# Four weight sums of a seven-product pair on VectorE, and a planner rule for the port that it shares with GpSimd

## The chip, the core and the metric

The kernel runs on one core of a Trainium2 chip. The metric is the device time of one execution in microseconds; for each kernel the median of the runs is given. Besides these there is one profiled execution, whose trace has the start and length of every instruction. Five engines work side by side, each through its own queue in order: TensorE (PE; its weight loads are listed apart as PEld), VectorE (DVE), ScalarE (ACT), GpSimd (POOL) and SyncE (SP), which here issues the DMA transfers.

## The reference

Two layers of an encoder on x (1, 512, 1024) in float32, with a memory of 256 tokens. Each layer adds three blocks to x:

```python
x += concat(neighbourhood_attention(h), gqa_attention(h)) @ w_out      # h = rms_norm(x)
x += memory_cross_attention(rms_norm(x), rms_norm(mem))                # 4 heads
x += conv_ffn(rms_norm(x))

def conv_ffn(h, w_up, conv_w, conv_b, w_down):
    u = h @ w_up                                   # (512, 2 x 2816)
    up = pad(u, one position on each side)
    u = up[:, :-2] * conv_w[0] + up[:, 1:-1] * conv_w[1] + up[:, 2:] * conv_w[2] + conv_b
    gate, val = split(u, 2)
    return (silu(gate) * val) @ w_down
```

A last RMSNorm follows. The change touches the product `h @ w_up` of the ConvFFN.

## The kernel before, in words

**Tiling.** x is kept transposed: eight tiles `xT` of 128 features by 512 positions. A float32 product is made exact enough by splitting both operands into a high part (a copy rounded to a TensorE format, on ScalarE) and a low part (operand minus high part, on VectorE or GpSimd), and issuing three matmuls: high by high, high by low, low by high. So every weight tile that a DMA brings as `raw` needs a copy and a subtraction before TensorE can use it.

**Seven products.** The hidden 2816 features make 22 blocks of 128. For each, gate and value are two products over 1024 features. Blocks 0 to 5 (`N_PLAIN = 6`) do them plainly. Blocks 6 to 21 do both at once as a two-by-two block product in Strassen's manner, with seven products of half the width instead of eight: 16 such pairs in each layer, 32 in all. `take_pair` fetches two raw weight tiles (128 x 1024 each), `combined` (L573 to L589) makes of them the seven weight operands: `11`, `12` and `22` are halves of the raw tiles, and four are sums,

```python
s1 = first[:, 4:8] + second[:, 0:4]        s3 = first[:, 0:4] + second[:, 0:4]
s2 = s3 + first[:, 4:8]                    s4 = s2 + second[:, 4:8]
```

each an add on 128 x 512 float32. All seven are then split (copy on ScalarE, subtraction on VectorE). `SUMS` (L506) names the engine of the four adds, GpSimd. `up` (L1603) issues the seven `product`s (L1589, 12 matmuls of 256 columns each) in the order 11, s1, s2, 12, s4, s3, 22; between them stand the matmuls of a block of the second FFN product, `down_grouped`, whose results are added into `xT`. `up_finish` (L1633) does convolution taps, SiLU and the product of the two sides on ScalarE and VectorE.

**Buffers.** `raw` has three slots (`N_RAW = 3`); the tiles `t` (sums among them) fourteen. A slot that comes free lets SyncE issue the next transfer.

**The order of the work.** No instruction is issued where it is written. Each call is put on a `Tape` as a `Step`, with its reads, writes, an estimated duration, and `shared`, which is true for GpSimd steps of more than 8 columns and for VectorE steps whose inputs are both in SBUF (and for some copies). `plan` lists candidate orders: it calls `run`, a list scheduler, with six settings of `PLANS` and four rounds each, replays each order six times with disturbed durations, and keeps the one with the least mean end. `play` then issues all steps in that order at one line (L405 of before, L408 of the changed kernel), so all rows of the profile have this line and are told apart by their tile names. An engine's order is thus fixed when the program is built.

In `run`, an engine's candidates are the steps whose inputs are done; each has an earliest start `t` from its data (`ready`), its engine (`free`) and free slots. Among those that could start within `patience` of the first, the one with the earliest due time is picked. When a `shared` step is picked while the other engine still has the port, it is lengthened by what is left of that, less `GRACE` (140 ns); `pool` and `vector` hold the end of the last shared step on GpSimd and VectorE.

Of the kernel before, what the change touches and what calls it, by code (L numbers as in the profile page):

```python
# [72 lines left out]
E_PE, E_ACT, E_DVE, E_POOL, E_SP = ENGINES  # L73
HANDOVER, LANDING, IN_FLIGHT, GRACE = 40.0, 1800.0, 8, 140.0
# [27 lines left out]
class Step:  # L102
# [5 lines left out]
    def __init__(self, i, engine, name, call, args, kwargs):  # L108
        self.i, self.engine, self.name, self.call = i, engine, name, (call, args, kwargs)
        self.reads, self.writes = [], []  # L110
        for n, a in [*enumerate(args), *kwargs.items()]:
            if hasattr(a, "tensor") or type(a).__name__ == "Tile":
                a = a if hasattr(a, "ap") and not callable(a.ap) else a[:]
                (self.writes if n in (0, "out", "accum_out") else self.reads).append(a)
        self.needs, self.frees, self.after, self.leads = set(), set(), set(), set()
        self.opens, self.tiles, self.moved = [], [], 0
        if name == "dma_start":
            self.busy = self.length = 450.0
            to, source = self.writes[0], self.reads[0] if self.reads else None
            runs = min(run(a) for a in (to, source) if a is not None)  # L120
            inside = source is not None and type(source.tensor).__name__ == type(to.tensor).__name__ == "Tile"
            rate = 205.0 if to.shape[0] < P or inside else 285.0 if runs < 256 else 340.0 if runs < 512 else 375.0
            self.moved = 4 / rate
            for c in to.shape:
                self.moved *= c
        elif name == "make_identity":
            self.busy = self.length = 1200.0
        else:
            self.busy, self.length = self.times()
        ends = self.reads[:: max(1, len(self.reads) - 1)] if name in TWO_INPUTS else self.reads[:1] + self.writes  # L130
        self.shared = engine == E_POOL and columns(self.writes[0]) > 8 or (
            engine == E_DVE and (name in TWO_INPUTS or name in FAST and (name == "tensor_copy" or columns(self.writes[0]) > 4))
            and all(tag_of(a.tensor) not in IN_PSUM for a in ends))
# [48 lines left out]
class Tape:  # L182
# [87 lines left out]
    def run(self, due, rank, patience, ahead, margin=0.0, aside={}, order=None, rng=None):  # L270


        steps = self.steps
        todo = [len(s.needs) + len(s.after) for s in steps]
        start, ready, free = [-1.0] * len(steps), [0.0] * len(steps), [0.0] * 5
# [14 lines left out]
        pool = vector = memory = 0.0  # L290
        flying = [0.0] * IN_FLIGHT

        def room(s):
            t = 0.0
            for x in s.opens:
                tag = self.tag[x]
                n = len(slots[tag])
                if not n or not order and x != waiting[tag][0] and (n <= aside.get(tag, n) or x not in waiting[tag][:5]):
                    return None
                t = max(t, min(slots[tag]))  # L300
            return t

        for _ in steps:
            best = None
            for e in ENGINES:
                if order or e == E_PE:
                    while head[e] < len(program[e]) and start[program[e][head[e]]] >= 0:
                        head[e] += 1
                    if head[e] == len(program[e]):
                        continue  # L310
                if order:
                    i = program[e][head[e]]
                    among = (i,) if not todo[i] else ()
                elif e == E_PE:
                    reach = rank[program[e][min(head[e] + ahead, len(program[e]) - 1)]]
                    among = [i for i in open_to[e] if rank[i] <= reach]
                else:
                    among = open_to[e]
                can = []
                for i in among:  # L320
                    t = room(steps[i]) if steps[i].opens else 0.0
                    if steps[i].moved and t is not None:
                        t = max(t, flying[-IN_FLIGHT])
                    if t is not None:
                        can.append((max(t, ready[i], free[e]), i))
                if can:
                    soon = min(can)[0] + patience[e]
                    _, t, i = min((due[i] if due and e != E_PE else rank[i], t, i) for t, i in can if t <= soon)
                    if best is None or t < best[0]:
                        best = t, i  # L330
            if best is None:
                return None
            t, i = best
            s = steps[i]
            busy = s.busy * slow[i]
            if s.shared and s.engine == E_POOL:
                busy += max(0.0, vector - t - GRACE)
                pool = t + busy
            elif s.shared:
                busy += max(0.0, pool - t - GRACE)  # L340
                vector = t + busy
            start[i], free[s.engine] = t, t + busy
            end = t + busy + s.length - s.busy + late[i]
            if s.moved:
                memory = max(memory, t + busy) + s.moved
                end = memory + LANDING + (12.0 * late[i] if rng is None else 1500.0 * rng.random())
                flying.append(end)
            taken.append(i)
            open_to[s.engine].remove(i)
            for x in s.opens:  # L350
                tag = self.tag[x]
                slots[tag].remove(min(slots[tag]))
                waiting[tag].remove(x)
            for x in s.tiles:
                left[x] -= 1
                ends[x] = max(ends.get(x, 0.0), end)
                if not left[x]:
                    slots[self.tag[x]].append(ends[x] + HANDOVER)
            for x in s.frees:
                q = steps[x]  # L360
                same = q.engine == s.engine and not s.moved
                ready[x] = max(ready[x], t if same and s.engine == E_PE else end + (30.0 if same else HANDOVER))
                todo[x] -= 1
                if not todo[x]:
                    open_to[q.engine].append(x)
            for x in s.leads:
                ready[x] = max(ready[x], t)
                todo[x] -= 1
                if not todo[x]:
                    open_to[steps[x].engine].append(x)  # L370
# [129 lines left out]
def encoder_kernel(ctx: ExitStack, tc: tile.TileContext, t: dict, out: list):  # L500
    nc = tc.nc
    tape = Tape()
    PE, ACT, DVE, POOL, SP = (
        Taped(tape, e, calls) for e, calls in zip(ENGINES, (nc.tensor, nc.scalar, nc.vector, nc.gpsimd, nc.sync)))
    late = Late(PE)
    LO_A, SUMS, LO_S = DVE, POOL, DVE  # L506
# [15 lines left out]
    def rtile(shape, dt=F32R):  # L522
        return rpool.tile([P, *shape], dt, tag="r", name=nm("r"), padded_shape=[P, *pad(shape)])
# [12 lines left out]
    def tmp(shape=(S,)):  # L536
        return tpool.tile([P, *shape], F32, tag="t", name=nm("t"))
# [13 lines left out]
    plan, raws, ready = [], [], []  # L551
# [15 lines left out]
    def operand_of(v, tile, sub):  # L567

        w = tile.rearrange("p (n k) c -> p n k c", n=2)
        ACT.copy(w[:, 0], v)  # L570
        sub.tensor_sub(w[:, 1], v, f(w[:, 0]))
        return [(w[:, 0, k], w[:, 1, k]) for k in range(4)]

    def wtile(tag):
        return wpool.tile([P, KC, P], F32R, tag=tag, name=nm(tag))

    def combined(first, second, early):

        parts = {}
        for n, v in (("11", first[:, 0:4]), ("12", second[:, 4:8]), ("22", first[:, 4:8])):  # L580
            parts[n] = operand_of(v, rtile((8, P)), LO_A)
        sums = {n: tmp((4, P)) for n in ("s3", "s1", "s2", "s4")}
        SUMS.tensor_add(sums["s1"], first[:, 4:8], second[:, 0:4])
        SUMS.tensor_add(sums["s3"], first[:, 0:4], second[:, 0:4])
        SUMS.tensor_add(sums["s2"], sums["s3"], first[:, 4:8])
        SUMS.tensor_add(sums["s4"], sums["s2"], second[:, 4:8])
        for n, tag in (("s1", "hi"), ("s2", "lo"), ("s4", "hi"), ("s3", "lo")):
            parts[n] = operand_of(sums[n], rtile((8, P)) if early else wtile(tag), LO_S)
        return parts  # L589
# [76 lines left out]
    first = nc.const_aps.tensor(0.0, (P, P), F32)  # L666
# [1299 lines left out]
```

## Time and profile before

| what | value |
|---|---|
| median of 3 runs | 1300.8 us (1300.58 to 1301.65) |
| span of the profiled execution | 1300.8 us |
| its own time | 1302.85 us |
| TensorE busy | 1290.8 us, 99% |
| VectorE busy | 1076.1 us, 83% |
| ScalarE busy | 784.4 us, 60% |
| GpSimd busy | 659.5 us, 51% |
| granted TensorE clock | 0.998 |

The span is the time between the first and the last instruction of the trace. A row of the timeline gives the start, the length in us, the engine, the line, the operation, output<-inputs by tile name, shapes, and the count of rows that were joined; in brackets the idle time of the engine just before, and what ended it. A row of a group gives total busy time, mean ns of one, idle time before, and its releaser. For the tile names: `mm`, `sc` and `tr` are PSUM banks, `r`, `hi`, `lo` and `xg` hold split operands, `t` and `s` are scratch.

### The profile page before, as it was taken

How to read it: one execution, taken by the hardware profiler on the slowest of the kernel's cores; microseconds unless marked ns; L12 is line 12 of the kernel's file. 1: busy time of each engine (PE TensorE's matmuls, PEld its weight loads, DVE VectorE, ACT ScalarE, POOL GpSimd, SP SyncE). 2: the span in 40 equal slices, each digit the busy share in tenths (PEclk: the TensorE clock that was granted, in tenths of full speed). 3: DMA queues.
4: the chain of work that ended last, by engine and by line, in shares of the span. 5: the costliest groups of instructions: out<-in, count | busy, mean ns of one | idle time of the engine just before them, and what ended most of it. 6: DMA issues, size and time to landing. Idle time of an engine off the chain costs nothing.

```text
span 1300.8 us, 20807 instructions
## 1 busy us (share of the span) xinstructions
PE 1290.8 (99%) x7557; PEld 1138.5 (88%) x7557; DVE 1076.1 (83%) x2001; ACT 784.4 (60%) x1526; POOL 659.5 (51%) x527
## 2 busy tenths in 40 slices
PE   9999999999999999999999999999999999999998
PEld 7898888888899999999888988888888999999997
DVE  7689885769999999888555897956799999997884
ACT  7776786555665555554537866865646555554552
POOL 4565857716823534433726566765365333452360
PEclk9999999999999999999999999999999999999999
DMA  8741313313224333223355322232132233323231
GB/s 286 224 141 49 105 56 98 98 35 113 81 82 123 105 113 115 66 98 123 112 162 179 115 80 82 65 99 96 49 98 81 82 115 115 128 99 98 97 99 66
DMA packets 42902, 137.48 MB, mean 106 GB/s; under 512 B 5040, under 2 KB 8496, under 8 KB 42800
## 3 DMA queue, kind: packets, MB, share of 16 engines
q1 hardware_dynamic: 42224, 135.51, 32.9%
q8 instruction: 59, 0.97, 0.3%
q10 hardware_dynamic: 576, 0.66, 0.1%
q14 instruction: 43, 0.35, 0.1%
HBM read 126.18 MB, written 2.10 MB: 99 GB/s over the span
## 4 chain that ended last, share of the span: by engine, by line
PE 91%; DVE 5%; issue 2%; POOL 2%; ACT 1%; DVEq 0%; POOLq 0%; ACTq 0%
PE mm L405 52%; PE tr L405 20%; PE sc L405 19%; DVE t L405 2%; DVE r L405 1%; POOL lo L405 1%; DVE lo L405 0%; DVE s L405 0%; POOL s L405 0%; POOL t L405 0%; ACT r L405 0%; ACT t L405 0%; DVE mm L405 0%; DVE xg L405 0%; DVE hi L405 0%
## 5 line engine op out<-in xcount | busy, mean ns | idle before, releaser
L405 POOL TENSOR_TENSOR lo<-raw,hi 128x512 fp32r<-128x512 f32 (+2 forms) x164 | 255.9, 1579 | 161.6 <-ACT hi L405 153.9
L405 PE MATMUL mm<-xg,hi 128*128 128x512 f32 (+1 forms) x930 | 289.7, 392 | 0.0
L405 POOL TENSOR_TENSOR t<-raw,raw 128x512 f32<-128x512 f32 x64 | 99.1, 1569 | 284.2 <-DMA raw<-in_w 231.1
L405 ACT CAST hi<-raw 128x512 fp32r<-128x512 f32 (+2 forms) x212 | 159.6, 779 | 109.2 <-issue 37.2
L405 PE MATMUL mm<-r,hi 128*128 128x512 f32 (+1 forms) x704 | 222.0, 388 | 0.0
L405 PEld LDWEIGHTS mm<-xg,hi 128*128 128x128 f32 x930 | 170.8, 189 | 31.9
L405 PE MATMUL mm<-xg,lo 128*128 128x512 f32 (+1 forms) x465 | 181.3, 390 | 0.0
L405 PEld LDWEIGHTS mm<-r,hi 128*128 128x128 f32 x704 | 130.2, 188 | 25.9 <-DVE xg L405 0.8
L405 PE MATMUL mm<-r,lo 128*128 128x512 f32 (+1 forms) x384 | 141.5, 369 | 0.0
L405 PE MATMUL sc<-r,r 128*128 128x256 f32 (+1 forms) x760 | 133.9, 309 | 0.0
L405 PE MATMUL sc<-r,hi 128*128 128x256 f32 (+1 forms) x832 | 122.9, 291 | 0.8 <-DVE hi L405 0.8
L405 PEld LDWEIGHTS sc<-r,hi 128*128 128x128 f32 x832 | 109.0, 192 | 3.6 <-DVE hi L405 1.0
L405 PEld LDWEIGHTS sc<-r,r 128*128 128x128 f32 x760 | 106.0, 191 | 6.3 <-ACT t L405 0.6
L405 PE MATMUL tr<-r,lo 128*128 128x256 f32 (+1 forms) x784 | 108.9, 285 | 0.0
L405 PE MATMUL mm<-hi,xg 128*128 128x512 f32 (+1 forms) x384 | 108.1, 357 | 0.0
L405 POOL TENSOR_TENSOR t<-t,raw 128x512 f32<-128x512 f32 x64 | 102.7, 1605 | 5.0
L405 PEld LDWEIGHTS mm<-xg,lo 128*128 128x128 f32 x465 | 87.5, 188 | 18.2
L405 POOL TENSOR_SCALAR t<-t,s 128x512 f32<-128x512 f32 (+1 forms) x112 | 66.9, 611 | 71.7 <-DVE s L405 68.4
L405 PE MATMUL tr<-r,r 128*128 128x256 f32 x768 | 102.7, 283 | 0.0
L405 PEld LDWEIGHTS tr<-r,r 128*128 128x128 f32 x768 | 98.9, 191 | 2.6
L405 PEld LDWEIGHTS tr<-r,lo 128*128 128x128 f32 x784 | 99.7, 192 | 0.8
L405 DVE TENSOR_TENSOR r<-raw,r 128x512 fp32r<-128x512 f32 x96 | 91.3, 956 | 0.2 <-ACT r L405 0.2
(160 smaller groups left out, 2697.3 us busy)
## 6 DMA issues: line engine op xcount, KB each, us to landing
raw<-in_w SPq DMA_DIRECT2D x207, 512.0 KB, 3.5
r<-r SPq DMA_DIRECT2D x30, 256.0 KB, 3.6
r<-in_bias SPq DMA_DIRECT2D x16, 384.0 KB, 4.6
raw<-in_w SPq DMA_DIRECT2D x8, 384.0 KB, 3.1
r<-in_memT SPq DMA_DIRECT2D x4, 512.0 KB, 6.7
xT<-in_w SPq DMA_DIRECT2D x7, 256.5 KB, 4.5
r<-in_w SPq DMA_DIRECT2D x9, 128.0 KB, 4.1
t<-in_memT SPq DMA_DIRECT2D x4, 256.0 KB, 6.1
```

The costliest lines, as they stand in the source:

```text
L405: call(*args, **kwargs)
```

## The change

The four adds of `combined` are written for VectorE instead of GpSimd. In the scheduler, the earliest start of a `shared` candidate now includes the end of the other engine's last shared step, less `GRACE`, while an order is being made (not in the replays, which have an `order`). The lengthening of a picked step stays as it is.

```diff
@@ run, the candidates of an engine @@
                     if t is not None:
-                        can.append((max(t, ready[i], free[e]), i))
+                        t = max(t, ready[i], free[e])
+                        if not order and steps[i].shared:
+                            t = max(t, (vector if e == E_POOL else pool) - GRACE)
+                        can.append((t, i))
                 if can:
                     soon = min(can)[0] + patience[e]
@@ combined @@
-        SUMS.tensor_add(sums["s1"], first[:, 4:8], second[:, 0:4])
-        SUMS.tensor_add(sums["s3"], first[:, 0:4], second[:, 0:4])
-        SUMS.tensor_add(sums["s2"], sums["s3"], first[:, 4:8])
-        SUMS.tensor_add(sums["s4"], sums["s2"], second[:, 4:8])
+        DVE.tensor_add(sums["s1"], first[:, 4:8], second[:, 0:4])
+        DVE.tensor_add(sums["s3"], first[:, 0:4], second[:, 0:4])
+        DVE.tensor_add(sums["s2"], sums["s3"], first[:, 4:8])
+        DVE.tensor_add(sums["s4"], sums["s2"], second[:, 4:8])
```

Both parts re-make the order of the whole program. TensorE has the same matmuls, in the same order through the steady pairs; 128 rows leave GpSimd's queue for VectorE's.

The first place is VectorE's queue at the start of the kernel (26 us in the profile). `t_107` is a sum of squares over the features, `s_129` its reduction, on which TensorE's `tr_130` waits; `lo_121` is the low part of a weight tile. Before:

```order
L405 TENSOR_TENSOR t_107<-t_107,t_113 128x512
L405 TENSOR_TENSOR lo_121<-raw_115,hi_120 128x512
L405 STREAM_TRANSPOSE t_128<-t_107 128x512
L405 TENSOR_TENSOR lo_121<-raw_115,hi_120 128x512
L405 TENSOR_REDUCE s_129<-t_128 128x16
```

And now:

```order
L408 TENSOR_TENSOR t_107<-t_107,t_113 128x512
L408 TENSOR_TENSOR lo_121<-raw_115,hi_120 128x512
L408 STREAM_TRANSPOSE t_128<-t_107 128x512
L408 TENSOR_REDUCE s_129<-t_128 128x16
L408 TENSOR_TENSOR lo_121<-raw_115,hi_120 128x512
```

The second half of the low part has moved behind the reduction. On TensorE, `tr_130` stands three matmuls earlier.

The second place is VectorE's queue at the end of layer 0 (650 to 655 us), where the last `xT_79` is closed: `xg_1242` is an operand of the next layer's first products, `t_1260` again a sum of squares whose reduction is `s_1294`. Before:

```order
L405 COPY xT_79<-mm_1282 128x512
L405 TENSOR_TENSOR t_1260<-t_1260,t_1286 128x512
L405 SCALAR_TENSOR_TENSOR xg_1242<-mm_1282,par,xg_1241 128x512
L405 STREAM_TRANSPOSE t_1293<-t_1260 128x512
L405 TENSOR_REDUCE s_1294<-t_1293 128x16
```

And now:

```order
L408 COPY xT_79<-mm_1282 128x512
L408 SCALAR_TENSOR_TENSOR xg_1242<-mm_1282,par,xg_1241 128x512
L408 TENSOR_TENSOR t_1260<-t_1260,t_1286 128x512
L408 STREAM_TRANSPOSE t_1293<-t_1260 128x512
L408 TENSOR_REDUCE s_1294<-t_1293 128x16
```

The operand `xg_1242` has moved ahead of the add.

The third place is VectorE's queue at the second pair of layer 1 (1018 to 1026 us). `raw_1996` and `raw_2009` are the pair's raw tiles, `r_...<-raw` their splits, `t_2036` is s1 and `hi_2039` its low part, which TensorE's second product reads; `t_2035` is s3, `t_2037` s2. Before:

```order
L405 TENSOR_TENSOR r_2032<-raw_1996,r_2032 128x512
L405 SCALAR_TENSOR_TENSOR t_2019<-mm_1997,par,t_2019 128x504
L405 SCALAR_TENSOR_TENSOR t_2020<-mm_2010,par,t_2020 128x504
L405 TENSOR_TENSOR tr_2029<-tr_2029,t_2031 128x256
L405 TENSOR_TENSOR r_2033<-raw_2009,r_2033 128x512
L405 SCALAR_TENSOR_TENSOR t_2019<-mm_1997,par,t_2019 128x7
L405 SCALAR_TENSOR_TENSOR t_2020<-mm_2010,par,t_2020 128x7
L405 TENSOR_TENSOR t_2017<-t_2017,t_2018 128x512
L405 TENSOR_TENSOR hi_2039<-t_2036,hi_2039 128x512
```

And now:

```order
L408 TENSOR_TENSOR r_2032<-raw_1996,r_2032 128x512
L408 SCALAR_TENSOR_TENSOR t_2019<-mm_1997,par,t_2019 128x504
L408 SCALAR_TENSOR_TENSOR t_2020<-mm_2010,par,t_2020 128x504
L408 TENSOR_TENSOR t_2036<-raw_1996,raw_2009 128x512
L408 TENSOR_TENSOR t_2035<-raw_1996,raw_2009 128x512
L408 TENSOR_TENSOR tr_2029<-tr_2029,t_2031 128x256
L408 TENSOR_TENSOR t_2037<-t_2035,raw_1996 128x512
L408 TENSOR_TENSOR hi_2039<-t_2036,hi_2039 128x512
L408 TENSOR_TENSOR r_2033<-raw_2009,r_2033 128x512
```

Three of the four adds are now in this queue ahead of `hi_2039`, and a raw split, two short taps' products and the product of the activations have moved behind it.

On GpSimd's queue in the memory stage of layer 1 (782 to 788 us) one half of a weight's low part (`lo_1597`) has moved from ahead of the scaling of two attention tiles (`t_1565`, `t_1566`), which TensorE then transposes, to behind it.

## The prediction

> **What bounds the kernel now.** I read the busy shares first, then the waits of TensorE, then the stage that the change edits.
>
> ```profile
> PE 1290.8 (99%) x7557; PEld 1138.5 (88%) x7557; DVE 1076.1 (83%) x2001; ACT 784.4 (60%) x1526; POOL 659.5 (51%) x527
> PE 91%; DVE 5%; issue 2%; POOL 2%; ACT 1%; DVEq 0%; POOLq 0%; ACTq 0%
> ```
>
> TensorE is busy for 1290.8 of 1300.8 us and the chain that ended last runs through it for 91%. A change that leaves its matmuls alone can win only where TensorE waits. The view of waits, for TensorE over the whole span, lists those (its own sequencer's row left out):
>
> ```profile
> PE tr L405 <- DVE s L405: 1.2, 1, 1.2
> ...
> PE tr L405 <- POOL t L405: 0.5, 1, 0.5
> PE tr L405 <- DVE r L405: 0.4, 1, 0.4
> ```
>
> With the two `sc` rows that are worked out below (0.8 and 0.2 us) that is 3.1 us in five places, each hit once. None lies in the steady pairs of the feed-forward block, where the four sums run. The windows of two such pairs (15.54 us is the distance from one pair's first product to the next's) and of fourteen in a row show it; the columns are PE, PEld, DVE, ACT, POOL, granted clock, DMA share and GB/s:
>
> ```profile
> 391.12:406.66 15.54, 15.54 (x110) 14.58 (x109) 15.54 (x25) 8.10 (x14) 6.32 (x5) 1.00 0.43 131
> 406.66:422.20 15.54, 15.54 (x110) 14.58 (x109) 15.22 (x26) 8.74 (x16) 4.80 (x4) 1.00 0.37 116
> 375.58:593.14 217.56, 217.56 (x1493) 203.20 (x1492) 204.35 (x316) 117.85 (x208) 88.39 (x58) 1.00 0.33 106
> ```
>
> TensorE fills every pair, VectorE is busy for 204.35 of 217.56 us. So VectorE has 13.2 us over in fourteen pairs, 0.94 us in each, and work is to be added to it: this is the place to be careful.
>
> **The change, part one: 128 adds move.** Four adds in each of 16 pairs and two layers leave GpSimd; the page's two groups (the first of two that read the raw weights, the second of one sum and a raw weight) are exactly these:
>
> ```profile
> L405 POOL TENSOR_TENSOR t<-raw,raw 128x512 f32<-128x512 f32 x64 | 99.1, 1569 | 284.2 <-DMA raw<-in_w 231.1
> L405 POOL TENSOR_TENSOR t<-t,raw 128x512 f32<-128x512 f32 x64 | 102.7, 1605 | 5.0
> ```
>
> GpSimd loses 201.8 us; in the pair shown next it has nothing else. What an add costs on VectorE has no row, but VectorE runs adds and subtractions of the same 128x512 operands. The timeline of one pair, GpSimd's two rows first:
>
> ```profile
> 405.66 2.55 POOL L405 TENSOR_TENSOR t<-raw,raw 128x512 f32<-128x512 f32 x2 [9.07 <-DMA raw<-in_w]
> ...
> 408.29 3.33 POOL L405 TENSOR_TENSOR t<-t,raw 128x512 f32<-128x512 f32 x2
> ...
> 410.39 1.78 DVE L405 TENSOR_TENSOR t<-t,t 128x512 f32<-128x512 f32 x1
> ...
> 413.40 1.60 PE L405 MATMUL sc<-r,hi 128*128 128x256 f32 x12
> ...
> 413.89 0.68 DVE L405 TENSOR_TENSOR hi<-t,hi 128x512 fp32r<-128x512 f32 x1
> ...
> 414.49 0.68 DVE L405 TENSOR_TENSOR xg<-t,xg 128x512 fp32r<-128x512 f32 x1
> ...
> 415.09 1.22 DVE L405 TENSOR_TENSOR lo<-raw,hi 128x1024 fp32r<-128x1024 f32 x1
> ```
>
> With GpSimd idle, the operations at 413.89, 414.49 and 415.09 last 0.68 us and start 0.60 apart: an add takes 0.60 us of the queue, four take 2.4 us a pair. Against that, VectorE's operations on two SBUF operands are stretched while GpSimd works: the product at 410.39 takes 1.78 us, and ends just after GpSimd's pair does (408.29 + 3.33 = 411.62). The groups of VectorE over 13 pairs (391.1 to 593.1 us) give the sum of that stretching:
>
> ```profile
> L405 DVE TENSOR_TENSOR r<-raw,r 128x512 fp32r<-128x512 f32 x39 | 37.3, 962 | 0.0
> L405 DVE TENSOR_TENSOR hi<-t,hi 128x512 fp32r<-128x512 f32 x26 | 25.1, 964 | 5.0 <-ACT hi L405 5.0
> ...
> L405 DVE SCALAR_TENSOR_TENSOR t<-sc,par,t 128x504 f32<-128x504 f32 x27 | 19.9, 735 | 1.1 <-ACT t L405 1.0
> L405 DVE TENSOR_TENSOR lo<-t,lo 128x512 fp32r<-128x512 f32 x26 | 18.9, 738 | 0.1
> L405 DVE TENSOR_TENSOR lo<-raw,hi 128x1024 fp32r<-128x1024 f32 x14 | 18.8, 1346 | 0.1
> ...
> L405 DVE TENSOR_TENSOR xg<-t,xg 128x512 fp32r<-128x512 f32 x11 | 13.3, 1213 | 0.0
> L405 DVE TENSOR_TENSOR t<-t,t 128x512 f32<-128x512 f32 x13 | 11.1, 853 | 0.1
> ...
> L405 DVE SCALAR_TENSOR_TENSOR t<-sc,par,t 128x7 f32<-128x7 f32 x27 | 5.9, 217 | 0.0
> L405 DVE TENSOR_TENSOR tr<-tr,t 128x256 f32<-128x256 f32 x13 | 5.5, 426 | 1.7 <-PE tr L405 1.7
> ```
>
> The taps' products (`t<-sc,par,t`) and `tr<-tr,t`, on PSUM, are not stretched. Over the undisturbed 0.68 us (1.22 for the wide one) the excess of the others is 39 x 0.282 + 26 x 0.284 + 26 x 0.058 + 14 x 0.126 + 11 x 0.533 + 13 x 0.173 = 29.8 us, 2.3 us a pair. In a steady pair 2.4 us of adds thus stand against 2.3 us of stretching that goes with GpSimd's work: the load stays at 14.6 to 14.7 of 15.54 us, TensorE remains the bound, and this part is worth **0.0** in the 32 pairs. What hides the adds is the 15.54 us of matmuls; without that cover they cost what rival three says. The Trainium skill ("SBUF — State Buffer", section "SBUF: two separate sides") calls the pair of ports that GpSimd and VectorE share an exclusive lock, with the loser blocked for the whole instruction; the 1.78 us agree, and by it all of the 2.3 us should go.
>
> New in the queue: an add waits for the second raw tile's landing, and behind it stand VectorE's splits and the taps' products. GpSimd waited 9.07 us for that tile and nobody stood behind it. The first sum is used by TensorE at 413.40 at the earliest; with the landing at 405.66, tap products and two adds ahead, its split ends near 411.3, 2 us early. So a landing as in this trace costs nothing, which I take; one later by more than 2 us would (rival three).
>
> **Part two: the planner's order.** In the new order the matmuls of the steady pairs stand as before; the places where TensorE waits are re-ordered. One after the other, what was late and what now stands ahead:
>
> At 26 us (the start):
>
> ```profile
> 24.54 1.15 DVE L405 TENSOR_TENSOR lo<-raw,hi 128x512 fp32r<-128x512 f32 x1
> ...
> 25.61 0.67 DVE L405 TENSOR_REDUCE s<-t 128x16 f32<-128x512 f32 x1
> ...
> 26.34 0.40 PE L405 MATMUL tr<-s,sel 128*128 128x16 f32 x2 [1.23 <-DVE s L405]
> ```
>
> The second `lo` goes behind the reduce, which then starts 1.07 us earlier (25.61 - 24.54); TensorE's consumer also moves three matmuls (0.68 us) up, so not all is won. Bounds 0 and -1.2 (the wait) with 0.16 of slower restart, -1.4; I take **-1.1**, near the 1.07.
>
> At 653 us (end of layer 0):
>
> ```profile
> 650.48 2.25 DVE L405 TENSOR_TENSOR t<-t,t 128x512 f32<-128x512 f32 x1 [0.77 <-ACT t L405]
> ...
> 652.66 0.74 DVE L405 SCALAR_TENSOR_TENSOR xg<-mm,par,xg 128x512 fp32r<-128x512 f32 x1
> ...
> 653.45 0.50 PE L405 MATMUL sc<-xg,hi 128*128 128x512 f32 x1 [0.22 <-DVE xg L405]
> ...
> 654.02 0.63 PE L405 MATMUL sc<-xg,hi 128*128 128x512 f32 x2
> ...
> 654.79 0.39 PE L405 MATMUL tr<-s,sel 128*128 128x16 f32 x2
> ```
>
> The add of 2.25 us, held by GpSimd, goes behind `xg`, which is then there 2 us before it is used. 0.22 us of wait and 0.11 of slow restart (0.50 against 0.39) go. 654.79 - 654.02 is 0.77 where two matmuls take 0.48 (0.63 for two less 0.39 for one, twice): 0.3 more, lost to the sum of squares `s`. The stretched add can end when it does now, but what follows it is rid of the 0.74 of `xg`, so `s` comes some 0.7 earlier. Bounds -0.2 and -0.6; I take **-0.6**.
>
> At 786 us (memory stage, layer 1):
>
> ```profile
> 782.15 3.79 POOL L405 TENSOR_TENSOR lo<-raw,hi 128x512 fp32r<-128x512 f32 x3
> ...
> 786.67 0.65 PE L405 MATMUL tr<-ident,t 128*128 128x128 f32 x4 [0.47 <-POOL t L405]
> ```
>
> One of the three splits (3.79 / 3 = 1.26 us) goes behind the scaling that TensorE awaits: 1.26 us earlier against 0.47 of wait and 0.15 of restart. Bounds 0 and -0.6; I take **-0.6**.
>
> At 1025 us (second pair of layer 1, in front of the first steady pairs):
>
> ```profile
> 1024.11 0.40 PE L405 MATMUL sc<-r,hi 128*128 128x256 f32 x2
> ...
> 1024.62 0.68 DVE L405 TENSOR_TENSOR hi<-t,hi 128x512 fp32r<-128x512 f32 x1
> 1025.35 1.46 PE L405 MATMUL sc<-r,hi 128*128 128x256 f32 x10 [0.85 <-DVE hi L405]
> ```
>
> Both parts work here: no GpSimd add stretches VectorE, and the split `hi` stands ahead of a raw split and the product of the activations, each 1.5 us now. Even with three adds (1.8 us) ahead it comes about 2.3 us earlier, before 1024.35. 1025.35 - 1024.11 is 1.24 where two matmuls take 0.24: **-1.0**, bounds 0 and -1.0.
>
> The 0.4 us behind `r` (at 122 us) are not touched. A re-made order of some twenty thousand instructions has waits of its own that the old one did not have; the old one's are 3.1 us, so between 0 and +3.1, and I take **+0.9**, the lower third, since GpSimd's load falls by 201.8 us and nothing else is added.
>
> Sum: 0.0 - 1.1 - 0.6 - 0.6 - 1.0 + 0.9 = -2.4 us. The profiled execution's span is 1300.8 us (1302.85 us by its own timing), the median of the runs shown is 1300.8, so both give **1298.4 us**.
>
> **Rivals.** *One: every wait goes and no new one comes*: 0.0 - 1.4 - 0.6 - 0.6 - 1.0, and the 0.4 at 122 us: -4.0, 1296.8. For it: less stretching everywhere. Against: an order is never free of waits at stage borders.
>
> *Two: the planner's rule has no net effect*, as its new picks lose at other borders what they win: 1299.8 to 1302, about 1300.8. For it: the rule changes which step is picked, not any cost, and the reference of 3.1 us is small; GpSimd still splits weights in the attention stages.
>
> *Three, the other side: VectorE's queue is held at an add by the raw tile.* The place is the first add of a pair, the price what the landing is late beyond the 2 us, and it decides from there, since VectorE has only 0.9 us a pair to catch up. For it: 231.1 us of GpSimd's idle time, 3.6 us for each of 64, went to this tile. Against: the same transfers are issued as early, and the DMA share is 0.37 to 0.43. Late by 0.2 to 0.5 us net in each of 32 pairs: +6 to +16, about 1307.
>
> *Four: VectorE becomes the bound*, because operations do not overlap once they depend on one another. By whole durations a pair would be 16 operations of 0.68 (the four adds among them), four taps' products of 0.735, four of 0.217, one of 0.426 and one of 1.22: 16.3 us against 15.54, 0.8 x 32 = +25, 1326. Against it: rows above start 0.60 apart with 0.68 of duration, and by the same count the pair before would be 16.3 - 4 x 0.68 + 2.3 = 15.9 us, more than TensorE's 15.54, which it never let wait. The Trainium skill ("VectorE: DVE Perf Modes", section "The DRAIN you can't avoid") says that the next operation does not start until the pipeline is empty, which would make this the case; the rows at 413.89 and 414.49 overlap, so I hold to them.
>
> **How the numbers follow.** Forecast (1297.0 to 1299.8) 0.52, rival one (1295.5 to 1297) 0.18, rival two 0.18, rival three 0.08, rival four 0.04. Range 1296.2 to 1301.8: it leaves out a part of rival one and all of three and four. 0.2%, 2.6 us, is about what a measurement here tells from no change: faster is below 1298.2, slower above 1303.4. Faster: 0.18 and 0.24 of the forecast's 0.52, 0.42; slower 0.13, the last two and a little of rival two; the same 0.45.
>
> **What would show it.** Right: VectorE's rows of 128x512 in steady pairs all near 0.68 us, four adds among them, its busy time in fourteen pairs near 205 us, TensorE still full there; the waits at 26, 653, 786 and 1025 us gone. Wrong: a TensorE wait for a VectorE split in the pairs, VectorE waiting for the raw tile ahead of an add, or new waits at stage borders of over 1 us together.

## The result and the profile after

The changed kernel takes 1299.43 us (median of 22 runs, 1298.78 to 1300.41), the kernel before on the same chips 1301.45 us (22 runs, 1300.22 to 1303.69). The ratio is 0.9984, with a 95% interval of 0.9977 to 0.9990: 2.0 us faster, where 2.4 was forecast. The runs of the kernel before are spread over 3.5 us, those of the changed one over 1.6; the profiled execution of before (1302.85 us by its own time) was one of its longer ones.

The page of the changed kernel, busy shares; then its view of TensorE's waits (total in us, times, longest), its sequencer's row left out:

```profile
PE 1289.2 (99%) x7557; PEld 1138.2 (88%) x7557; DVE 1063.4 (82%) x2129; ACT 782.2 (60%) x1526; POOL 467.1 (36%) x399
```

```profile
PE tr L408 <- POOL t L408: 0.6, 1, 0.6
PE sc L408 <- ACT xg L408: 0.4, 1, 0.4
PE tr L408 <- POOL s L408: 0.4, 1, 0.4
PE tr L408 <- DVE s L408: 0.3, 1, 0.3
PE tr L408 <- DVE mem_rep L408: 0.2, 1, 0.2
PE mm L408 <- DVE xg L408: 0.2, 1, 0.2
PE tr L408 <- DVE r L408: 0.2, 1, 0.2
```

GpSimd's 128 adds are on VectorE's account, 192 us of GpSimd are gone, and TensorE's waits are 2.3 us in place of 3.1: the two large ones (1.2 and 0.8) have given way to several small ones. The window of the same fourteen pairs, columns as before:

```profile
375.58:593.14 217.56, 217.56 (x1496) 203.33 (x1495) 204.35 (x370) 118.28 (x208) 0.00 (x0) 1.00 0.32 101
```

VectorE has 54 instructions more (370 against 316) and is busy for the same 204.35 us. The groups of VectorE in 13 pairs say how:

```profile
L408 DVE TENSOR_TENSOR r<-raw,r 128x512 fp32r<-128x512 f32 x39 | 26.7, 696 | 2.0 <-ACT r L408 2.0
...
L408 DVE TENSOR_TENSOR hi<-t,hi 128x512 fp32r<-128x512 f32 x26 | 18.0, 693 | 0.7 <-ACT hi L408 0.7
L408 DVE TENSOR_TENSOR t<-t,raw 128x512 f32<-128x512 f32 x26 | 18.0, 691 | 0.0
...
L408 DVE TENSOR_TENSOR t<-raw,raw 128x512 f32<-128x512 f32 x24 | 16.1, 691 | 0.7 <-DMA raw<-in_w 0.7
...
L408 DVE TENSOR_TENSOR xg<-t,xg 128x512 fp32r<-128x512 f32 x10 | 7.0, 695 | 0.0
```

The raw splits went from 962 to 696 ns, `xg` from 1213 to 695, and the four adds, 691 ns each, fill what that left. They wait for a raw tile for 0.7 us in all.

Where the 2.9 us are by which TensorE's last matmul starts earlier (1291.59 against 1294.47 us from the span's start) can be read from the starts of consecutive matmuls: the time lost beyond the usual distance (227 ns for 512 columns, 120 for 256), summed by place. The sums differ by 2.75 us. These are figures of two single executions:

| place | before, us | after, us | forecast |
|---|---|---|---|
| 25 to 50 us | 1.57 | 0.61 | -1.1 |
| 650 to 675 us | 0.97 | 0.17 | -0.6 |
| 775 to 800 us | 1.58 | 1.58 | -0.6 |
| 1000 to 1050 us | 1.39 | 0 | -1.0 |
| all steady pairs | 0 | 0 | 0.0 |
| everything else | 14.69 | 15.09 | +0.9 |
| sum | 20.20 | 17.45 | -2.4 |

### The profile page after: what moved, and what is told of

The parts are those of the page before. It is cut to its first block, busy times and chain, and to the rows that moved or that the text cites. A ratio compares the mean times of both kernels' runs of the same rounds, so it can differ in the third digit from the quotient of the medians.

```text
span 1298.2 us, 20665 instructions
## 1 busy us (share of the span) xinstructions
PE 1289.2 (99%) x7557; PEld 1138.2 (88%) x7557; DVE 1063.4 (82%) x2129; ACT 782.2 (60%) x1526; POOL 467.1 (36%) x399
## 4 chain that ended last, share of the span: by engine, by line
PE 94%; DVE 2%; DMA 1%; POOL 1%; ACT 1%; issue 1%; SPq 0%; POOLq 0%; DVEq 0%; ACTq 0%
PE mm L408 55%; PE tr L408 20%; PE sc L408 19%; POOL lo L408 1%; DMA t<-in_memT 1%; DVE t L408 0%; DVE r L408 0%; SPq L408 0%; DMA raw<-in_w 0%; ACT t L408 0%; DMA r<-in_w 0%; POOL s L408 0%; DVE s L408 0%; POOL t L408 0%; DVE xg L408 0%
## 5 line engine op out<-in xcount | busy, mean ns | idle before, releaser
L408 ACT ACTIVATE t<-sc,s,s 128x512 f32<-128x512 f32 (+1 forms) x96 | 68.0, 709 | 28.9 <-DVE s L408 28.4
L408 PEld LDWEIGHTS mm<-r,lo 128*128 128x128 f32 x384 | 72.3, 188 | 12.5
L408 ACT CAST hi<-t 128x512 fp32r<-128x512 f32 x64 | 39.8, 622 | 61.7 <-DVE t L408 35.3
```

The source lines that it names most:

```text
L408: call(*args, **kwargs)
```

## The experiments

**Each part alone.** `adds_only` has the four adds on VectorE and the old picking rule:

```diff
-                        t = max(t, ready[i], free[e])
-                        if not order and steps[i].shared:
-                            t = max(t, (vector if e == E_POOL else pool) - GRACE)
-                        can.append((t, i))
+                        can.append((max(t, ready[i], free[e]), i))
```

(against the changed kernel); `rule_only` is the kernel before with these lines the other way round. Expected:

> The four adds on VectorE, the planner's picking rule as before. The traces of before and after put the 2.9 us by which the last matmul comes earlier to four places: 0.9 us at 26 us, 0.7 at 653 us, 1.4 near 1025 us, and the rest spread. Theory one (each part has its own place: the adds mend only the pair at 1025 us, the picking rule the queue at 26 us): in this kernel the low part is again ahead of the reduction at 26 us and the add ahead of the operand at 653 us, so these waits stay (1.2 us and 0.2 us, and 0.3 lost to the reduction), the 0.85 us wait at 1025 us is gone; 0.8 to 1.4 us faster than before, 1300.0 to 1300.7 on the scale where before is 1301.4. Rival (the adds are worth nothing, the whole gain is the planner's): no difference to before within 0.5 us. Rival (the adds are the gain, the rule is nothing): 2.0 us faster, as the changed kernel.

> The picking rule alone, the four adds on GpSimd. Theory one (each part has its own place): the order at 26 us and at 653 us is that of the changed kernel, so the waits there are gone (0.9 and 0.7 us), the pair at 1025 us still has GpSimd's adds stretching VectorE, so a wait of about 0.8 us stays there: 1.2 to 1.7 us faster than before. Rival (adds are the gain): no difference within 0.5 us. Rival (the rule is the whole gain): 2.0 us faster.

Measured: `adds_only` 1301.02 us, ratio to before 0.9996 (0.9987 to 1.0005), no difference that can be told; `rule_only` 1299.59 us, 0.9987 (0.9978 to 0.9996). So with the planner as it is, the whole gain comes with the rule, and none with the adds. Theory one had 0.8 to 1.4 us for the adds and 1.2 to 1.7 for the rule; measured are 0.4 and 1.9. The places do not follow it either. In `rule_only`, GpSimd still makes the sums, and nothing is lost at the second pair of layer 1. Its timeline:

```profile
1016.69 0.42 DVE L408 TENSOR_TENSOR tr<-tr,t 128x256 f32<-128x256 f32 x1
1016.70 2.66 POOL L408 TENSOR_TENSOR t<-t,raw 128x512 f32<-128x512 f32 x2
...
1017.28 0.68 DVE L408 TENSOR_TENSOR sc<-sc,t 128x512 f32<-128x512 f32 x1
...
1017.88 1.51 DVE L408 SCALAR_TENSOR_TENSOR t<-mm,par,t 128x504 f32<-128x504 f32 x3
...
1020.04 0.67 DVE L408 TENSOR_TENSOR hi<-t,hi 128x512 fp32r<-128x512 f32 x1
...
1021.98 1.60 PE L408 MATMUL sc<-r,hi 128*128 128x256 f32 x12
```

While GpSimd adds (1016.70 to 1019.36), VectorE is given work with an operand in PSUM, which is not stretched (0.68 us, as alone), and `hi` is there 1.3 us early. In fourteen pairs this kernel's VectorE is busy for 193.37 us with the same instructions as before (204.35): the rule takes a third of the 2.3 us of stretching per pair away (0.8 us a pair). TensorE is busy throughout this window either way, so no time comes of it here.

```profile
375.58:593.14 217.56, 217.56 (x1497) 203.38 (x1496) 193.37 (x316) 117.27 (x208) 82.10 (x55) 1.00 0.32 104
```

And in `adds_only` the order at 653 us is that of before (the add ahead of `xg`), yet the place loses 0.17 us, not 0.97. Its timeline:

```profile
649.38 4.26 POOL L405 TENSOR_TENSOR lo<-raw,hi 128x512 fp32r<-128x512 f32 x3
...
651.50 0.99 DVE L405 TENSOR_TENSOR t<-t,t 128x512 f32<-128x512 f32 x1 [0.77 <-ACT t L405]
652.41 0.74 DVE L405 SCALAR_TENSOR_TENSOR xg<-mm,par,xg 128x512 fp32r<-128x512 f32 x1
```

The add comes 2.1 us behind the first of GpSimd's three splits, as in before, but takes 0.99 us and not 2.25, and the three splits take 4.26 and not 3.81: by these lengths VectorE seems to have got the port between two of them here, and GpSimd to have waited. The same rows in the same order thus came out differently.

**Is it the rule, or the order that is drawn?** The planner tries six settings and keeps the order that its own replays like best. In the kernel before the second setting wins (patience 60, margin 120 ns), in the changed kernel and in `rule_only` the third (60, 160), in `adds_only` the fifth (120, 120). So these comparisons mix an edit with a change of setting. Held to one setting by

```diff
-PLANS = [... for patience in (60.0, 120.0) for margin in (80.0, 120.0, 160.0)]
+PLANS = [... for patience in (60.0, 120.0) for margin in (80.0, 120.0, 160.0)][1:2]
```

(`[2:3]` for the third), each edit can be seen alone:

> Neither part of the change: the kernel before, with the planner held to its third setting (patience 60, margin 160 ns), which is the one that wins in the changed kernel, while its second (60, 120) wins in the kernel before. Theory two (a part of the gain belongs to neither edit, but to the other setting that the planner's judgement happens to choose): the order at 653 us is here that of the changed kernel (the operand ahead of the add) and at 26 us that of before, so the 0.7 us at 653 us are won and the 1.2 us wait at 26 us stays: 0.5 to 1.0 us faster than before, if no new wait comes with it. Theory one without this: as before, or up to 1.3 us slower, as the planner's own judgement has it.

> Both parts of the change, with the planner held to its second setting (patience 60, margin 120 ns), the one that wins in the kernel before. The order at 26 us has the reduction ahead of the low part, that at 653 us the add ahead of the operand as before, and at 1025 us three adds on VectorE. Theory two (the gain at 653 us belongs to the setting): TensorE waits at 653 us as before (0.2 us, and 0.3 to the reduction), nowhere at 26 and 1025 us; 1.2 to 1.6 us faster than before, 0.5 to 0.8 slower than the changed kernel. Rival (the setting is nothing): 2.0 us faster than before.

> Adds on VectorE, old picking rule, the planner held to its second setting, that of the kernel before. So beside the kernel before only the four adds differ. Theory three (the moved adds are worth nothing by themselves; what an edit does to the time is which order it happens to draw, and its one-off waits): within 1.5 us of before on either side, no TensorE wait in the steady pairs, and the low part ahead of the reduction at 26 us as before, so the wait of about 1.2 us stays there. Theory one (the adds mend the pair at 1025 us): 1.0 to 1.4 us faster.

> Adds on VectorE, old picking rule, the planner held to its third setting. The kernel before with this setting took 1303.7 us and waited in pairs (near 350 and 1000 us) on ScalarE's results, with GpSimd's adds stretching VectorE; the changed kernel with it took 1299.4, the picking rule alone 1299.6. Theory four (in this setting the contention for the port is what costs, and either part of the change removes it): near 1300, 3 us or more faster than before with this setting. Theory three (order's luck): anywhere from 1299 to 1304. If the picking rule were the only cure: near 1303.7.

> The picking rule alone, the planner held to its second setting. With this setting before took 1301.45 and both parts 1302.1. The order at 26 us has the reduction ahead, at 653 us the add ahead. Theory one (each wait that is re-ordered is won): no wait at 26 us, 0.8 us faster than before. Theory three (the gain depends on the draw, other waits come): 1300 to 1303, TensorE's waits at other stage borders add up to 2 us or more, as with both parts (3.2 us).

Measured, median in us and ratio to the kernel before run beside it, with its interval:

| | second setting | third setting |
|---|---|---|
| neither part | 1301.45 (the kernel before) | 1303.68; 1.0013 (1.0004 to 1.0022) |
| adds alone | 1300.22; 0.9990 (0.9982 to 0.9999) | 1304.43; 1.0023 (1.0014 to 1.0032) |
| rule alone | 1305.80; 1.0029 (1.0018 to 1.0040) | 1299.59; 0.9987 (the run above) |
| both | 1302.10; 1.0001 (0.9993 to 1.0010) | 1299.43; 0.9984 (the changed kernel) |

The rule makes the kernel 4.1 and 5.0 us faster in the third setting (1303.68 to 1299.59, 1304.43 to 1299.43) and 4.4 and 1.9 us slower in the second. The adds go from 3.7 us faster to 0.8 slower. These are differences of medians from separate comparisons, in which the kernel before took 1301.45 and 1301.85 us; by the ratios in the table the rule is 3.4 and 5.1 us faster in the third setting and 3.8 and 1.4 slower in the second, with the same signs. Neither part has a worth of its own that holds over the settings; the theory of places falls, and so does theory four for the adds. Theory two falls too: the kernel before with the third setting was to be 0.5 to 1.0 us faster and is 2.2 slower, and both parts with the second were to be 1.2 to 1.6 faster and show no difference. The rule alone with the second setting lies above every figure named for it. Theory one's figure came true once, for the adds in the second setting (1.0 to 1.4 us forecast, 1.3 by the ratio): the 1.39 us near 1025 us are gone there. But so are 0.8 us at 650 us, where the order is that of before.

What the rule was made for does hold over the settings: VectorE's busy time in the fourteen pairs falls from 204.35 to 190.18 us in the second and from 203.53 to 193.37 in the third, with GpSimd's adds in place. What the rule cures in TensorE's waits in the third setting is in the trace: neither part and adds alone lose 0.9 to 1.0 us at 350 to 375 and again at 1000 to 1025 us, where TensorE waits for ScalarE's `t` (the row of TensorE's waits of neither part, then that of the adds alone):

```profile
PE sc L405 <- ACT t L405: 2.4, 4, 0.8
```

```profile
PE sc L405 <- ACT t L405: 2.2, 4, 0.6
```

With the rule this row is gone, and nothing is lost at the two places. In the second setting other waits stand in the traces with the rule; that they make up its loss is not shown. With both parts it is GpSimd's small vector `s` at 30 us:

```profile
30.14 0.40 PE L408 MATMUL tr<-s,sel 128*128 128x16 f32 x2 [1.48 <-POOL s L408]
```

with the rule alone a transfer at 81 us (this profiled execution, 1310.25 us, was longer than that kernel's median by 4.4 us, so its rows are not the median's):

```profile
81.09 0.74 PE L408 MATMUL sc<-r,r 128*128 128x256 f32 x4 [3.23 <-DMA r<-r]
```

**A wait at a stage border is not a property of the order alone.** `adds_setting2` gives a control that I had not planned. Its queues are, row by row, those of the kernel before until the seven products are prepared (the first rows of VectorE, GpSimd and ScalarE that differ stand at 349 to 353 us in the trace of before). So at 26 us it is the same program; there the second `lo` is ahead of the reduction, as in before, and still TensorE does not wait. Its timeline:

```profile
24.02 1.15 DVE L405 TENSOR_TENSOR lo<-raw,hi 128x512 fp32r<-128x512 f32 x1
25.09 0.67 DVE L405 TENSOR_REDUCE s<-t 128x16 f32<-128x512 f32 x1
...
25.88 0.34 PE L405 MATMUL tr<-s,sel 128*128 128x16 f32 x2
```

The place loses 0.32 us here and 1.57 in the profiled execution of before. The reduction starts 0.5 us earlier (25.09 against 25.61), which alone would leave 0.7 of the 1.23 us of wait. The larger part is that TensorE itself comes 0.92 us later (the two matmuls ahead of `tr` start at 25.42 against 24.50): it had already waited at 10 us, for a copy on ScalarE that stood behind a later landing of `xT`. The timeline of `adds_setting2`, then that of before:

```profile
9.17 0.72 ACT L405 ACTIVATE xg<-xT 128x512 fp32r<-128x512 f32 x1 [1.45 <-DMA xT<-in_w]
...
10.24 0.81 PE L405 MATMUL sc<-xg,hi 128*128 128x512 f32 x2 [0.88 <-ACT hi L405]
```

```profile
8.11 0.73 ACT L405 ACTIVATE xg<-xT 128x512 fp32r<-128x512 f32 x1 [0.50 <-DMA xT<-in_w]
...
9.45 1.08 PE L405 MATMUL sc<-xg,hi 128*128 128x512 f32 x4
```

So most of the wait at 26 us did not vanish but stood at 10 us; `tr` starts 0.46 us earlier (25.88 against 26.34), and that is all that this execution gained at this place. My 1.2 us at 26 us was one execution's.

**VectorE's room in a pair.** The first sum is computed twice and three times (`add_twice`, `add_thrice`) in each pair:

```diff
         DVE.tensor_add(sums["s1"], first[:, 4:8], second[:, 0:4])
+        DVE.tensor_add(sums["s1"], first[:, 4:8], second[:, 0:4])
```

> The changed kernel, with the first of the four sums computed twice in each of the 32 pairs (same result): one more add of 0.69 us on VectorE, 0.60 of its queue. My account of VectorE's load (14.7 of 15.54 us a pair, 0.8 us over) says that it is hidden: within 1.5 us of the changed kernel's 1299.4 (what a re-made order draws), no TensorE wait in steady pairs, and VectorE's idle time in the 13 pairs falls from about 13 to about 5 us. The count by whole durations (16.3 us a pair, VectorE already full) says +0.69 x 32 = +22 us.

> The changed kernel, with the first sum computed three times in each pair (same result): two more adds on VectorE. One more add took VectorE's busy time in fourteen pairs from 204.35 to 212.19 us, 0.56 us a pair, at no cost in time. Two more should need 220.0 of 217.56 us: TensorE then waits 0.18 us in each of 32 pairs, the kernel gets 4 to 8 us slower than with one more add (1304 to 1308), with waits of TensorE for VectorE in the steady pairs. If VectorE can lend work to the other stages, or my load is too high: still 1299 to 1301. By whole durations (0.69 each) it would be +0.35 x 32 = +11 us.

`add_twice`: 1299.63 us, ratio to before 0.9982 (0.9974 to 0.9991), as the changed kernel. `add_thrice`: 1302.72 us, 1.0006 (0.9997 to 1.0015). The fourteen pairs of the two:

```profile
375.58:593.14 217.56, 217.56 (x1497) 203.38 (x1496) 212.19 (x383) 119.32 (x208) 0.00 (x0) 1.00 0.32 102
```

```profile
375.58:593.14 217.56, 217.56 (x1485) 202.87 (x1484) 215.87 (x392) 117.00 (x205) 0.00 (x0) 1.00 0.32 100
```

One add more costs VectorE 7.84 us in fourteen pairs, 0.56 a pair, or 0.60 for each of the 13 instructions more that the window holds (383 against 370), and TensorE nothing: the count by whole durations is out. Two more fill VectorE to 99%. 1302.72 is less than I had expected (1304 to 1308). VectorE ran 9 instructions more in the window than with one add, not 13 or 14, so some work seems to slip behind, and TensorE's first wait behind the pairs is one of 1.2 us between 1250 and 1260 us. Its trace loses 3.5 us more than that of `add_twice`, 3.1 of them near 650, 750 and 1250 us (0.8, 1.2 and 1.1), so two thirds of it are again stage borders away from the pairs. The edge of VectorE's room lies near two more adds; where exactly, this run doesn't settle.

**The port's price.** In `sums_on_both` GpSimd makes four adds of raw weights in every pair besides, into a tile that is never read (extra work; VectorE's own is unchanged):

```diff
+        spare = tmp((4, P))
+        POOL.tensor_add(spare, first[:, 4:8], second[:, 0:4])
+        POOL.tensor_add(spare, first[:, 0:4], second[:, 0:4])
+        POOL.tensor_add(spare, first[:, 0:4], first[:, 4:8])
+        POOL.tensor_add(spare, first[:, 4:8], second[:, 4:8])
```

> The changed kernel, and GpSimd computes four adds of raw weights in each pair besides, into a tile that nobody reads: the port's price without any change in VectorE's own work. In the kernel before such adds stretched VectorE by 2.3 us a pair, with the new picking rule alone by 1.6 (193.37 us in fourteen pairs, with 33 us less of adds, against 204.35). VectorE at 14.6 us a pair has 0.9 over: the excess is 0.7 to 1.4 us a pair, +22 to +45 us, 1321 to 1345, with waits of TensorE in steady pairs. If the planner can hide the port's conflicts (work on PSUM while GpSimd has the port): below 1305.

1342.37 us, ratio to before 1.031 (1.0296 to 1.0324): 43 us slower than the changed kernel, 1.3 us a pair, at the upper end of what was expected. Its window, one row of VectorE's groups in 13 pairs, and the first rows of TensorE's waits:

```profile
375.58:593.14 217.56, 207.01 (x1380) 189.60 (x1380) 209.48 (x348) 107.45 (x192) 81.25 (x52) 1.00 0.30 95
```

```profile
L408 DVE TENSOR_TENSOR t<-raw,raw 128x512 f32<-128x512 f32 x24 | 26.7, 1111 | 0.0
```

```profile
PE tr L408 <- ACT lo L408: 6.0, 8, 1.2
PE mm L408 <- ACT hi L408: 5.6, 2, 2.8
PE sc L408 <- DVE hi L408: 3.4, 6, 1.2
```

VectorE's adds are stretched from 691 to 1111 ns. TensorE waits in the pairs, and there mostly for the copies (ScalarE) and splits (VectorE) of the sums, `lo` and `hi`: 5.8 of the 8.8 us of waits that the view lists from 375 to 594 us. The two waits of 2.8 us are not in the pairs: they stand right behind each layer's last pair, where `hi` is a copy of a raw weight. VectorE is not full (209 of 217.56 us), so its load alone doesn't explain the price; that the chain from add to copy to split is stretched is my reading of these waits and not tested by itself. The extra tile and the three raw slots, which GpSimd now holds too, are part of this price; they weren't taken apart.

**Other draws with the change.** The changed kernel held to the sixth setting, and to one that isn't on the list:

> The changed kernel, with the planner held to its sixth setting (patience 120, margin 160 ns); by the planner's own estimate 0.6 us behind the third that it chooses. Theory three (the draw of an order decides within some us, and the planner's estimate does not see it): anywhere from 1298.5 to 1303, with other one-off waits than the changed kernel at stage borders. If the estimate could be trusted: 1299.5 to 1300.5.

> The changed kernel, with a setting of the planner that is not on its list (patience 60, margin 200 ns), which by the planner's own estimate is 0.2 us better than the best on the list. Theory three: anywhere from 1298.5 to 1303. If the estimate could be trusted: 1299.0 to 1299.5, a little better than the changed kernel.

1299.37 us, 0.9986 (0.9977 to 0.9995), and 1299.66 us, 0.9985 (0.9976 to 0.9994). Both are as fast as the changed kernel and none is better, though their profiled spans (1296.1 and 1296.6 us) are shorter than its 1298.2: a difference of 2 us between two single executions was no difference in the medians. With both parts, then, three of four settings give 1299.4 to 1299.7 and one gives 1302.1. The planner's own estimate doesn't rank them: it puts the second setting, the slowest by 2.4 us, 0.2 us behind the third, and the sixth 0.6 us behind. No version here beats the changed kernel.

## Why the prediction was right, and where it was not

**The steady pairs, 0.0**: right. VectorE's load is 204.35 us before and after; an add costs 0.56 to 0.60 of its queue (0.60 forecast, from starts 0.60 apart), and the stretching of 2.3 us a pair is what it replaced. The rule of the Trainium skill that I set against this ("VectorE: DVE Perf Modes", section "The DRAIN you can't avoid") is that the next operation does not start until the pipeline is empty. Taken alone it would have made VectorE the bound, and one more add would have cost an estimated 22 us (0.69 us of whole duration in each of 32 pairs); the trace does not agree, it cost nothing. The same section adds that an operation which is not held starts earlier, and rival four left that out. The exclusive lock of the Trainium skill ("SBUF — State Buffer", section "SBUF: two separate sides") fits the 1111 against 691 ns; a mean of 24 rows can't tell a lock from a shared port.

**Rival three** (VectorE held at an add by the raw tile): it did not happen. The 231.1 us that GpSimd waited for raw tiles were room and no lateness; VectorE's adds wait for 0.7 us in 13 pairs, because the planner puts them where the tile has landed.

**The four places, -1.1, -0.6, -0.6, -1.0**: the traces show -0.96, -0.80, 0.00 and -1.39, a sum of -3.15 against -3.3, which is close. The reasons were worse than the sum. At 786 us the wait moved with its consumer. The changed kernel's timeline:

```profile
781.48 2.56 POOL L408 TENSOR_TENSOR lo<-raw,hi 128x512 fp32r<-128x512 f32 x2
...
784.00 1.38 POOL L408 TENSOR_SCALAR t<-t,s 128x512 f32<-128x512 f32 x2
...
784.76 0.66 PE L408 MATMUL tr<-ident,t 128*128 128x128 f32 x4 [0.56 <-POOL t L408]
```

One split fewer stands ahead, 1.26 us as I said. But TensorE reached this place 1.5 us earlier than before, GpSimd's queue ahead of the splits only 0.7 us earlier (781.48 against 782.15), and the transpose stands two matmuls (0.45 us) earlier in TensorE's order: 1.26 - 0.8 - 0.45 is nothing. The step that failed is "1.26 us earlier against 0.47 of wait": I looked at the producer's queue and not at where the planner put the consumer, though I had done so at 26 us.

At 1025 us I wrote that both parts work. Either suffices in the kernels as planned: nothing is lost there in `adds_only` or `rule_only`. With the third setting the adds alone still lose 0.9 us between 1000 and 1025 us, to a result of ScalarE. At 653 us the swap isn't needed (`adds_only`). At 26 us it is neither needed (the kernel before with the third setting keeps the second `lo` ahead of the reduction and does not wait there) nor enough (both parts with the second setting have the swap, and TensorE waits 1.48 us for the next small vector).

**New waits, +0.9**: +0.4 in the trace, with small waits at 82, 92 and 820 us among them; one at 30 us is inside the first place's figure. Together the waits that are new come to 1.5 us in the view, and the wait at 786 us is still there (0.6 us). I had named new waits of over 1 us together as a sign of being wrong, so by my own signs the account of part two did not hold, though the time did.

**Rival two** (the rule has no net effect, as its picks lose elsewhere what they win) is the one that I set too low. In this kernel the time fell, and more than the interval; but over two settings the rule's effect is -5.0 to +4.4 us, and its sign hangs on the setting. The forecast of 1298.4 came within 1.0 us by luck in part: the waits that a new order has (2.3 us) and the old one had (3.1 us) are of one size, three of the four places that I counted happened to be mended, and the planner happened to choose a setting in which the rule gains. Why the second setting suits the old rule and the third the new one stays open.

## What to carry to other kernels

Work can move to an engine that is 94% busy at no cost, if moving it ends a contention that filled that engine: sum the stretching from a group's mean against its undisturbed duration, and set it against the added work by starts, not by durations. When an edit makes a planner re-make the order, compare at several of the planner's settings with and without the edit before believing that the edit did it; here the same rule was worth 5.0 us less or 4.4 us more depending on the setting, while the whole change was worth 2.0. And a wait of about 1 us at a stage border in one trace may be that execution's: with equal queues up to there, TensorE waited 1.2 us at 26 us in one execution, and in another not there but 0.9 us at 10 us. So add up the waits ahead of a place before calling one mended.

## What I had not expected of the hardware

VectorE was filled to 99% of a pair stage (215.87 of 217.56 us) without TensorE waiting in it. Where GpSimd made four adds besides, the loss was 43 us, 1.3 us a pair on average (the waits right behind the last pairs included), although VectorE's undisturbed load left 0.9 us a pair and its busy time even then was 96%.
